# A latent-attention and pooling block: per-token factors as rows, queries and keys of three head pairs kept on chip, first chunk by halves

## The chip, the cores and the metric

The kernel runs on one core of one Trainium2 chip. The metric is the device time of one execution in microseconds (us). The core's engines each run their own stream of instructions in order: TensorE (PE, with weight loads shown as PEld), VectorE (DVE), ScalarE (ACT), GpSimd (POOL) and SyncE (SP, whose queue issues nearly all DMAs). They wait for each other on semaphores.

## What is computed

One encoder layer on 1024 tokens of width 1024, in float32. The parts:

```python
def reference(x, norm_in, w_in, q_norm, w_uq, kv_norm, w_ukv, pool_w, pool_scale,
              w_branch_attn, w_branch_pool, w_out, norm_final):
    h = x
    for _ in range(DEPTH):
        hn = rms_norm(h, norm_in)
        z = jnp.einsum('bsd,de->bse', hn, w_in)
        zq, zkv, zkr, g_attn, u_pool, g_pool, g_merge = jnp.split(z, IN_SPLITS, axis=-1)
        y_attn = mla_attention(zq, zkv, zkr, q_norm, w_uq, kv_norm, w_ukv) * jax.nn.silu(g_attn)
        y_pool = multiscale_pool(u_pool, pool_w, pool_scale) * jax.nn.silu(g_pool)
        a = jnp.einsum('bsc,cd->bsd', y_attn, w_branch_attn)
        p = jnp.einsum('bsc,cd->bsd', y_pool, w_branch_pool)
        gate_a, gate_p = jnp.split(jax.nn.sigmoid(g_merge.astype(jnp.float32)).astype(h.dtype), 2, axis=-1)
        merged = gate_a * a + gate_p * p
        h = h + jnp.einsum('bsd,de->bse', merged, w_out)
    return rms_norm(h, norm_final)
```

`mla_attention` takes the normed latents zq (384 wide) and zkv (256 wide), makes for 8 heads queries and keys of 64 columns each ("nope") and 32 rotary columns, and attends causally by chunks of 64 tokens. `rms_norm` divides each token by its root mean square and multiplies by a gain.

## The kernel before

Every array on chip has features in its 128 partitions and the 1024 tokens in its columns (up to the last stage). A float32 product is made of three products of rounded parts: each operand is split into a high part (a ScalarE cast) and a low part (a VectorE subtraction, helper `split`), and PE adds high times high, high times low and low times high.

**What sets the order.** Nothing is issued where the code stands. The code records operations with the tiles that they read and write in a `Plan` (L85 to 206); `Plan.order` then schedules them by a model of costs, and each engine gets its stream in that order. Of the operations of an engine that could start within 30 ns of the first one, it takes the one recorded earliest. A row of a stream waits only for what it uses, but nothing passes a row that waits. SBUF tiles of 4 KB in each partition come from 45 slots of tag "t" and are handed out in the order of the code; raw weights of the small items have one buffer (tag "wr"), split weights two (tags "wh", "wl"). Each DMA of SP's queue takes one of eight completion semaphores in turn, so at most eight are under way.

**The stages** (times of the profiled execution):

- Up to about 58 us: eight warm-up matmuls, then the latents zq from eight chunks of the features (loop over `ORDER`, L604), each chunk with three products for two halves of the tokens and three column groups. A chunk is `x`; for the first four chunks `xa` holds the gain-scaled high and low part of tokens 0 to 511, `xb` those of the others; the first chunk is loaded and split by halves. Then the rotary key (`run_kr`) and zkv (`run_zkv`).
- `tokens` (L712) turns the sums of squares of the tokens, which lie in a [128 x 8] cell (token 128c + p in row p, column c), into a factor for each token. `spread` (L668) makes of such a cell a [128 x 1024] tile that has each token's factor in every partition: eight PE transposes of one column, broadcast to 128x128, into two PSUM banks. For `rstd`, ScalarE copies the banks to SBUF.
- 71 to 350 us: the rest of the input projection, in `Pair` items (seven products of a Strassen scheme each, 12 matmuls of 512 columns a product). Their weights `w_z` are split beside them. In the last gate pair stand two `Latents` items: they load zq and zkv back, multiply them by their tokens' factors (`spread`, straight from PSUM) and split them.
- 340 to 394 us: `run_up` makes queries and keys of a head pair p = 0 to 3 (64 + 64 partitions), split into `uh` and `ul`. These are stored to DRAM (`qn_d`, `kn_d`), and `load_head` loads the 64 rows of a head from there into the operand tiles `qh`, `ql`, `kh`, `kl` (rows 0 to 63; 64 to 95 rotary from `qr_d` and `kr_d`, 96 to 127 a mask). There are two such sets of tiles, `heads[h % 2]`; head 0's rows come straight from the tiles. `run_rope` and `run_v` follow.
- 394 to about 567 us: attention, head by head: scores `sc`, exponentials `pr` (ScalarE, with the row sums in `small`), transposes `pt`, their split `pT`, products `o` and their copies `oa`. Between them, as filler for PE, stand the products `pf` of the pooling branch (`run_branch_p`): weights `w_bp`, one of eight at a time into `wr`, cast to `wh`, rest to `wl`.
- Then the attention branch, the output projection in pieces, and `Rows.finish` (L1289), which scales the rows by their norm and stores them.

Of the kernel before, what the change touches and what calls it, by code (L numbers as in the profile page):

```python
# [14 lines left out]
P = 128  # L15
# [6 lines left out]
KV_RANK = 256  # L22
N_BG = 4
WARM = 8
# [185 lines left out]
def hybrid_block_kernel(  # L210
# [42 lines left out]
    def dram(rows, name, cols=T):  # L253
        b = Buf(lambda: tc.dram_tile([rows, cols], F32, name=name), None)
        return View(b, 0, rows, 0, cols)
# [219 lines left out]
    qr_d = [[dram(P, f"qr_d{t}{i}") for i in range(2)] for t in range(2)]  # L475
    qn_d = [[dram(P, f"qn_d{p}{i}") for i in range(2)] for p in range(4)]
    kn_d = [[dram(P, f"kn_d{p}{i}") for i in range(2)] for p in range(4)]
    gate_d = [dram(P, f"gate_d{t}") for t in range(16)]
# [125 lines left out]
    for n, k in enumerate(ORDER):  # L604
# [22 lines left out]
        h, l = xs[k]  # L627
        for a, b, f, e in ((wh, h, n == 0, False), (wh, l, False, False), (wl, h, False, n == 7)):
            for hf in range(2):
                mms([(zq_acc[c].halves[hf], a[:, 128 * c : 128 * c + 128], b[hf], f, e) for c in range(3)])  # L630
    for n in range(4):
# [35 lines left out]

    def spread(t, kind=None):  # L668
        acc = Acc(kind) if kind else next_acc()
        transposes(  # L670
            [
                (
                    acc.halves[c // 4][:, 128 * (c % 4) : 128 * (c % 4) + 128],
                    t[:, c : c + 1].via(lambda a: a.to_broadcast([P, P])),
                )
                for c in range(8)
            ]
        )
        return acc

# [31 lines left out]
    def tokens():  # L712
        ts(v_tok, v_tok, 1.0 / D, EPS, ALU.mult, ALU.add)
        inv_sqrt(r_tok, v_tok)
        a = spread(r_tok, "of")
        r = t32("rstd")
        for ps, c, d in a.spans:
            acopy(r[:, c:d], ps)
        state["r"] = r
        norm_tok("q", QK_DIM / Q_RANK, QK_DIM * EPS)  # L720
# [16 lines left out]
    class Latents:  # L737
# [4 lines left out]

        def load(self):
            self.z = [t32("z" + self.key) for _ in z_d[self.key]]
            for z, d in zip(self.z, z_d[self.key]):
                dma(z, d)

        def split(self):
            f = spread(f_tok[self.key], "of")
            for z in self.z:  # L750
                for ps, a, b in f.spans:
                    tt(z[:, a:b], z[:, a:b], ps, ALU.mult)
            state["c" + self.key] = [split_tile(z) for z in self.z]
# [57 lines left out]
    def load_head(h):  # L811
        d = heads[h % 2]
        p, r = h // 2, 64 * (h % 2)
        load_rope(h)
        for x, n in enumerate("hl"):
            dma(d["q" + n][0:64, :].f32(), qn_d[p][x][r : r + 64, :])
            dma(d["k" + n][0:64, :].f32(), kn_d[p][x][r : r + 64, :])

    def run_up(p, which, first):
        def run(it):  # L820
# [18 lines left out]
            for ps, a, b in acc.spans:  # L839
                split(h[:, a:b], l[:, a:b], ps)  # L840
            dst = qn_d if which == "q" else kn_d
            if p == 0:
# [3 lines left out]
                dma(heads[0][which + "l"][0:64, :].f32(), l[0:64, :].f32())  # L846
            r = 64 if p == 0 else 0
            dma(dst[p][0][r:P, :], h[r:P, :].f32())
            dma(dst[p][1][r:P, :], l[r:P, :].f32())
        return run  # L850
# [299 lines left out]
    gate_pair(12, [(3, Rotary())])  # L1150
    gate_pair(14, [(3, q), (5, kv)])
    for n, it in enumerate(i for i in items if isinstance(i, Pair)):
# [104 lines left out]
    class Rows:  # L1257
# [31 lines left out]
        def finish(self, e, last=False):  # L1289
# [12 lines left out]
            elif last:  # L1302
                act(r, r, AF.Copy, scale=st)
            else:
                stt(r, r, st, nf, ALU.mult, ALU.mult)
# [295 lines left out]
```

## Time and profile before

| | |
|---|---|
| three runs | 701.85, 703.6, 706.39 us; median 703.6 |
| profiled execution | 702.37 us |
| its span, first to last instruction | 700.2 us |
| mean granted clock of TensorE | 0.991 of full speed |
| busy: PE, DVE, ACT, POOL | 682.6, 539.6, 355.9, 116.8 us |
| moved by DMA | 136.42 MB |

The span is what the rows below lie in, with times from its start; 2.2 us of the profiled execution lie outside. An engine that is busy for nearly all of the span sets its length, up to the holes in its stream; where an engine waits, the row gives the idle time and what ended it. The clock is the share of full speed that PE was granted.

### The profile page before, as it was taken

How to read it: one execution, taken by the hardware profiler on the slowest of the kernel's cores; microseconds unless marked ns; L12 is line 12 of the kernel's file. 1: busy time of each engine (PE TensorE's matmuls, PEld its weight loads, DVE VectorE, ACT ScalarE, POOL GpSimd, SP SyncE). 2: the span in 40 equal slices, each digit the busy share in tenths (PEclk: the TensorE clock that was granted, in tenths of full speed). 3: DMA queues.
4: the chain of work that ended last, by engine and by line, in shares of the span. 5: the costliest groups of instructions: out<-in, count | busy, mean ns of one | idle time of the engine just before them, and what ended most of it. 6: DMA issues, size and time to landing. Idle time of an engine off the chain costs nothing.

```text
span 700.2 us, 9698 instructions
## 1 busy us (share of the span) xinstructions
PE 682.6 (97%) x3368; PEld 574.3 (82%) x3368; DVE 539.6 (77%) x868; ACT 355.9 (51%) x660; POOL 116.8 (17%) x153
## 2 busy tenths in 40 slices
PE   8999999999999999999999979999999999999995
PEld 6878888888888888888888769999899888878784
DVE  5687997668878578669958757877887889967883
ACT  5864524442444354443545546677676673334433
POOL 0020100300003030300001034444444300000000
PEclk9999999999999999999999989999999999999998
DMA  8947656361977539364778982554540389984612
GB/s 314 383 163 278 208 208 189 82 189 59 316 238 191 176 126 321 85 191 149 293 240 301 331 190 62 147 145 112 122 121 31 106 288 372 303 270 134 203 68 90
DMA packets 55871, 136.42 MB, mean 195 GB/s; under 512 B 5904, under 2 KB 17296, under 8 KB 55696
## 3 DMA queue, kind: packets, MB, share of 16 engines
q1 hardware_dynamic: 53568, 131.63, 56.0%
q0 software_dynamic: 2256, 4.20, 4.2%
q8 instruction: 26, 0.43, 0.3%
q14 instruction: 21, 0.17, 0.1%
HBM read 93.73 MB, written 46.27 MB: 200 GB/s over the span
## 4 chain that ended last, share of the span: by engine, by line
PE 88%; DMA 4%; DVE 3%; issue 2%; ACT 1%; SPq 1%; DVEq 0%; ACTq 0%
PE pb L275 36%; PE ps L275 31%; PE sc L275 6%; PE pf L275 5%; PE o L275 5%; PE pt L282 4%; PE pv L275 2%; DMA kh<-kr_d 1%; DMA wr<-w_bp 1%; SPq L378 1%; DMA x<-xT 1%; DVE mr L308 1%; DMA mr<-m_d 1%; DVE small L357 0%; DVE res L308 0%
## 5 line engine op out<-in xcount | busy, mean ns | idle before, releaser
L275 PE MATMUL pb<-t,wp 128*128 128x512 f32 x504 | 121.3, 389 | 0.0
L275 PEld LDWEIGHTS pb<-t,wp 128*128 128x128 f32 x504 | 94.4, 188 | 19.5
L298 ACT CAST wp<-wr 128x512 fp32r<-128x512 f32 x98 | 59.4, 620 | 94.6 <-PE ps L275 53.3
L308 DVE TENSOR_TENSOR wp<-wr,wp 128x512 fp32r<-128x512 f32 x98 | 71.9, 747 | 36.8 <-ACT wp L298 35.5
L275 PE MATMUL ps<-xa,wp 128*128 128x512 f32 x224 | 73.8, 389 | 0.0
L322 POOL TENSOR_SCALAR pr<-pr,small 128x128 f32<-128x128 f32 (+3 forms) x64 | 48.7, 765 | 77.3 <-DVE small L348 68.9
L290 ACT ACTIVATE pr<-sc,small 128x128 f32<-128x128 f32 (+3 forms) x64 | 47.6, 745 | 19.3 <-DVE small L357 16.4
L308 DVE TENSOR_TENSOR pT<-pt,pT 128x512 fp32r<-128x512 f32 (+1 forms) x80 | 48.8, 633 | 8.9 <-ACT pT L298 8.3
L357 DVE TENSOR_REDUCE small<-sc 128x1 f32<-128x128 f32 (+3 forms) x64 | 47.3, 750 | 9.8 <-PE sc L275 9.2
L298 ACT CAST pT<-pt 128x512 fp32r<-128x512 f32 (+1 forms) x80 | 41.5, 544 | 25.5 <-PE pt L282 24.5
L275 PE MATMUL o<-pT,v 128*128 128x256 f32 (+1 forms) x320 | 48.4, 286 | 2.0 <-ACT pT L298 1.5
L275 PEld LDWEIGHTS ps<-xa,wp 128*128 128x128 f32 x224 | 42.0, 188 | 8.7
L275 PEld LDWEIGHTS o<-pT,v 128*128 128x128 f32 x320 | 44.8, 193 | 4.8 <-ACT pT L298 1.9
L275 PE MATMUL ps<-xb,wp 128*128 128x512 f32 x112 | 43.6, 389 | 0.0
L282 PE MATMUL pt<-ident,pr 128*128 128x128 f32 x288 | 42.6, 276 | 0.3 <-DVE pT L308 0.3
L275 PE MATMUL pb<-wo,wp 128*128 128x512 f32 (+1 forms) x180 | 40.5, 376 | 0.2 <-DVE res L308 0.2
L275 PE MATMUL pb<-xa,wp 128*128 128x512 f32 x168 | 40.7, 389 | 0.0
L275 PE MATMUL ps<-t,wp 128*128 128x512 f32 x168 | 40.7, 390 | 0.0
L275 PE MATMUL sc<-kh,qh 128*128 128x384 f32 (+4 forms) x96 | 36.2, 377 | 2.9 <-ACT pr L290 2.8
L275 PEld LDWEIGHTS pb<-wo,wp 128*128 128x128 f32 x180 | 32.4, 188 | 7.0 <-issue 0.5
L275 PEld LDWEIGHTS pb<-xa,wp 128*128 128x128 f32 x168 | 31.5, 188 | 6.5
L275 PEld LDWEIGHTS ps<-t,wp 128*128 128x128 f32 x168 | 31.5, 188 | 6.5
(207 smaller groups left out, 1446.5 us busy)
## 6 DMA issues: line engine op xcount, KB each, us to landing
wr<-w_z SPq DMA_DIRECT2D x30, 512.0 KB, 5.3
gate_d<-z SPq DMA_DIRECT2D x16, 512.0 KB, 3.5
xt<-xr SPq DMA_DIRECT2D x8, 512.0 KB, 9.8
mp<-gate_d SPq DMA_DIRECT2D x8, 512.0 KB, 6.5
gate<-gate_d SPq DMA_DIRECT2D x8, 512.0 KB, 7.4
wo<-wt_d SPq DMA_DIRECT2D x8, 512.0 KB, 9.2
m_d<-gate SPq DMA_DIRECT2D x16, 256.0 KB, 5.7
mr<-m_d SPq DMA_DIRECT2D x16, 256.0 KB, 4.5
```

The source lines that it names most:

```text
L275: nc.tensor.matmul(real(o), real(a), real(b), start=s, stop=e, **kw)
L282: nc.tensor.transpose(real(o), real(a), real(ident))
L290: nc.scalar.activation(real(o), real(x), func, scale=real(scale), **kw)
L298: lambda: nc.scalar.copy(real(o), real(x)),
L308: plan.add(eng, lambda: e.tensor_tensor(real(o), real(a), real(b), op), c, [a, b], [o], port=port)
L322: e.tensor_scalar(real(o), real(a), real(s1), real(s2), op0, op1)
L357: lambda: nc.vector.tensor_reduce(real(o), real(a), axis=AX.X, op=ALU.max, negate=True),
L378: lambda: nc.sync.dma_start(real(o), real(x)),
```

## The change

Four things change.

1. `spread` makes one transpose of the [128 x 8] cell to [8 x 128], a ScalarE copy to a small tile `eight`, a store of its 4 KB to a new row in DRAM, and a load that repeats that row to all 128 partitions of a "t" tile. `rstd`, `fq` and `fkv` are made so, and multiplied with from SBUF, 1024 columns at a time. For a latent this now happens when it is loaded, not when it is split, and q stands one product earlier in the last gate pair.
2. For head pairs 0 to 2 (`KEPT`) `uh` and `ul` stay in their "t" tiles, and `load_head` copies from there; pair 3 goes through DRAM as before.
3. In the first chunk the loop over halves is outermost.
4. One of the last two row scalings moves from ScalarE to VectorE.

```diff
--- before.py
+++ after.py
@@ -20,7 +20,7 @@
 QK_DIM = 96
 Q_RANK = 384
 KV_RANK = 256
-N_BG = 4
+KEPT = 3
 WARM = 8
 SLOTS = {"t": 45, "wr": 1, "wh": 2, "wl": 2, "go": 2, "oa": 2, "s": 2, "p": 2, "o": 1, "f": 1}
 PSUM = "spof"
@@ -473,8 +473,8 @@
     mask_d = dram(64, "mask_d")
     kr_d = [dram(32, f"kr_d{i}") for i in range(2)]
     qr_d = [[dram(P, f"qr_d{t}{i}") for i in range(2)] for t in range(2)]
-    qn_d = [[dram(P, f"qn_d{p}{i}") for i in range(2)] for p in range(4)]
-    kn_d = [[dram(P, f"kn_d{p}{i}") for i in range(2)] for p in range(4)]
+    n_d = {w: [dram(P, f"{w}n_d{i}") for i in range(2)] for w in "qk"}
+    nope = {}
     gate_d = [dram(P, f"gate_d{t}") for t in range(16)]
     y_d = [dram(P, f"y_d{t}") for t in range(4)]
     gp_d = [dram(P, f"gp_d{t}") for t in range(4)]
@@ -625,9 +625,11 @@
         if n + 3 < 8:
             raws[ORDER[n + 3]] = start_loads(ORDER[n + 3])
         h, l = xs[k]
-        for a, b, f, e in ((wh, h, n == 0, False), (wh, l, False, False), (wl, h, False, n == 7)):
-            for hf in range(2):
-                mms([(zq_acc[c].halves[hf], a[:, 128 * c : 128 * c + 128], b[hf], f, e) for c in range(3)])
+        parts = ((wh, h, n == 0, False), (wh, l, False, False), (wl, h, False, n == 7))
+        for (a, b, f, e), hf in (
+            [(p, hf) for hf in range(2) for p in parts] if n == 0 else [(p, hf) for p in parts for hf in range(2)]
+        ):
+            mms([(zq_acc[c].halves[hf], a[:, 128 * c : 128 * c + 128], b[hf], f, e) for c in range(3)])
     for n in range(4):
         B.setdefault("b11", []).append((xs[n][0][0], xs[n][1][0]))
         B.setdefault("b21", []).append((xs[4 + n][0][0], xs[4 + n][1][0]))
@@ -665,18 +667,17 @@
         act(o, x, AF.Sqrt)
         recip(o, o)
 
-    def spread(t, kind=None):
-        acc = Acc(kind) if kind else next_acc()
-        transposes(
-            [
-                (
-                    acc.halves[c // 4][:, 128 * (c % 4) : 128 * (c % 4) + 128],
-                    t[:, c : c + 1].via(lambda a: a.to_broadcast([P, P])),
-                )
-                for c in range(8)
-            ]
-        )
-        return acc
+    def spread(t, name):
+
+        ps = Acc("of").halves[0]
+        transposes([(ps[:8, :P], t)])
+        eight = buf("oa", 256, F32, "eight")[:8, :P]
+        acopy(eight, ps[:8, :P])
+        d = dram(1, name)
+        dma(d.via(lambda a: a.rearrange("a (c p) -> (a c) p", c=8)), eight)
+        o = t32(name)
+        dma(o, d.via(lambda a: a.rearrange("a c -> (a c)").partition_broadcast(P)))
+        return o
 
     f_tok = {"q": cell(8), "kv": cell(8)}
     zq, zkv = [], []
@@ -712,11 +713,7 @@
     def tokens():
         ts(v_tok, v_tok, 1.0 / D, EPS, ALU.mult, ALU.add)
         inv_sqrt(r_tok, v_tok)
-        a = spread(r_tok, "of")
-        r = t32("rstd")
-        for ps, c, d in a.spans:
-            acopy(r[:, c:d], ps)
-        state["r"] = r
+        state["r"] = spread(r_tok, "rstd")
         norm_tok("q", QK_DIM / Q_RANK, QK_DIM * EPS)
 
     def run_zkv(j):
@@ -741,15 +738,14 @@
             self.key = key
 
         def load(self):
+            self.f = spread(f_tok[self.key], "f" + self.key)
             self.z = [t32("z" + self.key) for _ in z_d[self.key]]
             for z, d in zip(self.z, z_d[self.key]):
                 dma(z, d)
 
         def split(self):
-            f = spread(f_tok[self.key], "of")
             for z in self.z:
-                for ps, a, b in f.spans:
-                    tt(z[:, a:b], z[:, a:b], ps, ALU.mult)
+                tt(z, z, self.f, ALU.mult)
             state["c" + self.key] = [split_tile(z) for z in self.z]
 
         def go(self, it):
@@ -813,8 +809,8 @@
         p, r = h // 2, 64 * (h % 2)
         load_rope(h)
         for x, n in enumerate("hl"):
-            dma(d["q" + n][0:64, :].f32(), qn_d[p][x][r : r + 64, :])
-            dma(d["k" + n][0:64, :].f32(), kn_d[p][x][r : r + 64, :])
+            for w in "qk":
+                dma(d[w + n][0:64, :].f32(), nope[w, p][x][r : r + 64, :])
 
     def run_up(p, which, first):
         def run(it):
@@ -838,15 +834,17 @@
             h, l = tr("uh"), tr("ul")
             for ps, a, b in acc.spans:
                 split(h[:, a:b], l[:, a:b], ps)
-            dst = qn_d if which == "q" else kn_d
             if p == 0:
                 if which == "q":
                     make_slots()
                 dma(heads[0][which + "h"][0:64, :].f32(), h[0:64, :].f32())
                 dma(heads[0][which + "l"][0:64, :].f32(), l[0:64, :].f32())
-            r = 64 if p == 0 else 0
-            dma(dst[p][0][r:P, :], h[r:P, :].f32())
-            dma(dst[p][1][r:P, :], l[r:P, :].f32())
+            if p < KEPT:
+                nope[which, p] = h.f32(), l.f32()
+            else:
+                nope[which, p] = n_d[which]
+                for v, o in zip((h, l), n_d[which]):
+                    dma(o, v.f32())
         return run
 
     def run_rope(t):
@@ -1148,7 +1146,7 @@
     silu_pair(4, ga_d[2:4])
     gate_pair(10)
     gate_pair(12, [(3, Rotary())])
-    gate_pair(14, [(3, q), (5, kv)])
+    gate_pair(14, [(2, q), (5, kv)])
     for n, it in enumerate(i for i in items if isinstance(i, Pair)):
         for j, f in enumerate(hooks.get(n, [])):
             it.after[1 + 3 * j] = f
@@ -1300,7 +1298,7 @@
                 stt(r[:, 256:512], r[:, 256:512], st, nf[:, 256:512], ALU.mult, ALU.mult)
                 ts(r[:, :256], r[:, :256], st, None, ALU.mult)
             elif last:
-                act(r, r, AF.Copy, scale=st)
+                ts(r, r, st, None, ALU.mult)
             else:
                 stt(r, r, st, nf, ALU.mult, ALU.mult)
             for c in (lft, rgt):
```

**Where the instructions come to stand.** First PE's stream at its beginning: the 18 matmuls of the first chunk (`xa` holds the high and the low part of half 0, `xb` those of half 1, `wqh` and `wql` are the weights' parts; of the three accumulators `ps_130` and `ps_132` hold both halves, `pb_134` and `pb_146` one each). The piece of difference:

```order
 L275 MATMUL ps_132<-xa_121,wqh_126 128x512
 L275 MATMUL pb_134<-xa_121,wqh_126 128x512
+L275 MATMUL ps_130<-xa_121,wql_128 128x512
+L275 MATMUL ps_132<-xa_121,wql_128 128x512
+L275 MATMUL pb_134<-xa_121,wql_128 128x512
 L275 MATMUL ps_130<-xb_136,wqh_126 128x512
 L275 MATMUL ps_132<-xb_136,wqh_126 128x512
 L275 MATMUL pb_146<-xb_136,wqh_126 128x512
-L275 MATMUL ps_130<-xa_121,wql_128 128x512
-L275 MATMUL ps_132<-xa_121,wql_128 128x512
-L275 MATMUL pb_134<-xa_121,wql_128 128x512
 L275 MATMUL ps_130<-xb_136,wql_128 128x512
 L275 MATMUL ps_132<-xb_136,wql_128 128x512
```

The first nine matmuls, three with `xa`, three with `xb` and three with `xa` again (its low part), keep their order; behind them the three with `wql` for half 0 go ahead of the three for the low part of half 1.

Next SP's stream where attention begins, at the second load of `w_bp` into `wr` (the keys of the last pair are `uh_3179` and `ul_3191` before, `uh_3141` and `ul_3153` after), before:

```order
L378 DMA kn_d_3161<-uh_3146 128x1024
L378 DMA kn_d_3164<-ul_3148 128x1024
L378 DMA kn_d_3166<-uh_3150 128x1024
L378 DMA kn_d_3177<-ul_3153 128x1024
L378 DMA wr_3193<-w_bp 128x512
L378 DMA kn_d_3197<-uh_3179 128x1024
L378 DMA kn_d_3210<-ul_3191 128x1024
L378 DMA qh_3289<-mask_d 32x1024
```

and after:

```order
L378 DMA kl_3092<-kr_d_2663 32x1024
L378 DMA qn_d_3103<-ul_3075 128x1024
L378 DMA mp_3105<-gate_d_2265 128x1024
L378 DMA kl_3092<-ul_3088 64x1024
L378 DMA wr_3155<-w_bp 128x512
L378 DMA kn_d_3159<-uh_3141 128x1024
L378 DMA kn_d_3172<-ul_3153 128x1024
L378 DMA qh_3253<-mask_d 32x1024
```

Between the first load of `w_bp` and this second one stand nine issues now, seventeen before; what is gone are stores of `uh` and `ul`. The last pair's two key stores follow it in both. Then come head 1's ten loads, and behind them the third load of `w_bp`, before:

```order
L378 DMA ga_3299<-ga_d_2092 128x1024
L378 DMA qh_3289<-qr_d_3013 32x1024
L378 DMA ql_3293<-qr_d_3027 32x1024
L378 DMA qh_3289<-qn_d_2945 64x1024
L378 DMA kh_3291<-kn_d_3113 64x1024
L378 DMA ql_3293<-qn_d_2962 64x1024
L378 DMA kl_3295<-kn_d_3141 64x1024
L378 DMA wr_3359<-w_bp 128x512
L378 DMA qh_2928<-qr_d_3013 32x1024
```

and after:

```order
L378 DMA kh_3257<-uh_3077 64x1024
L378 DMA ql_3261<-qr_d_3005 32x1024
L378 DMA ql_3261<-ul_2912 64x1024
L378 DMA kl_3265<-kr_d_2663 32x1024
L378 DMA kl_3265<-ul_3088 64x1024
L378 DMA ga_3269<-ga_d_2087 128x1024
L378 DMA wr_3299<-w_bp 128x512
L378 DMA wr_3367<-w_bp 128x512
L378 DMA qh_2914<-qr_d_2991 32x1024
```

Head 1's rows 0 to 63 come from `uh` and `ul` and no longer stand at the end; the gate's load comes behind them, and the fourth load of `w_bp` follows the third at once.

Last ACT's stream at the same place: `wh<-wr` is the cast of a `w_bp` weight, `pr<-sc` an exponential, `pT<-pt` the cast of transposed probabilities, before:

```order
L298 CAST v_3287<-pv_3260 128x8x64
L290 ACT_TABLE_LOAD
L290 ACTIVATE pr_3323,small<-sc_3275,small 128x128
L290 ACTIVATE pr_3325,small<-sc_3279,small 128x256
L298 CAST wh_3334<-wr_3193 128x512
L298 CAST pT_3357<-pt_3348 128x384
L290 ACTIVATE pr_3364,small<-sc_3327,small 128x384
L290 ACTIVATE pr_3370,small<-sc_3336,small 128x512
L298 COPY oa_3386<-o_3374 64x256
```

and after:

```order
L298 CAST hi_3235<-y_2857 128x1024
L298 CAST wh_3246<-wr_3155 128x512
L298 CAST v_3251<-pv_3222 128x8x64
L290 ACT_TABLE_LOAD
L290 ACTIVATE pr_3287,small<-sc_3237,small 128x128
L290 ACTIVATE pr_3291,small<-sc_3241,small 128x256
L298 CAST pT_3321<-pt_3314 128x384
L290 ACTIVATE pr_3326,small<-sc_3293,small 128x384
L290 ACTIVATE pr_3332,small<-sc_3302,small 128x512
L298 CAST wh_3341<-wr_3299 128x512
L298 COPY oa_3350<-o_3336 64x256
```

The cast of the second weight now stands ahead of the table load and the exponentials, no longer ahead of `pT`; that of the third stands where attention's fourth exponential has been issued, ahead of `oa`.

## Rows read from the trace of the kernel before

**Rows 1.** The page, busy time of the engines: us, share of the span, instructions.

```profile
PE 682.6 (97%) x3368; PEld 574.3 (82%) x3368; DVE 539.6 (77%) x868; ACT 355.9 (51%) x660; POOL 116.8 (17%) x153
```

**Rows 2.** What PE waited for: total us, times, longest us.

```profile
PE sc L275 <- ACT pr L290: 2.8, 2, 2.0
PE o L275 <- ACT pT L298: 1.5, 1, 1.5
```

**Rows 3.** Timeline of ACT, first head: start, us, instruction, [idle before <-releaser].

```profile
394.94 1.28 ACT L290 ACT_TABLE_LOAD   x1
...
402.99 0.62 ACT L298 CAST wh<-wr 128x512 fp32r<-128x512 f32 x1 [4.93 <-DMA wr<-w_bp]
403.52 0.47 ACT L298 CAST pT<-pt 128x384 fp32r<-128x384 f32 x1
...
415.22 0.62 ACT L298 CAST wh<-wr 128x512 fp32r<-128x512 f32 x1 [3.55 <-DMA wr<-w_bp]
```

**Rows 4.** Timeline of PE, the same stretch, the rows with waits.

```profile
404.04 0.38 PE L275 MATMUL o<-pT,v 128*128 128x256 f32 x1 [1.53 <-ACT pT L298]
404.86 0.90 PE L275 MATMUL o<-pT,v 128*128 128x256 f32 x3 [0.43 <-DVE pT L308]
...
417.40 0.33 PE L275 MATMUL sc<-kh,qh 128*128 128x128 f32 x1 [1.97 <-ACT pr L290]
```

**Rows 5.** Stretches: us, busy of five engines, PEclk, DMA share, GB/s.

```profile
396.00:398.00 2.00, 2.00 (x10) 1.68 (x9) 1.58 (x5) 1.11 (x5) 0.05 (x1) 1.00 1.02 399
...
404.00:406.00 2.00, 1.53 (x6) 1.33 (x7) 1.61 (x5) 1.44 (x5) 1.00 (x2) 0.68 0.87 221
406.00:408.00 2.00, 2.00 (x9) 2.00 (x8) 0.93 (x3) 0.17 (x1) 0.28 (x1) 0.50 0.75 215
...
418.00:420.00 2.00, 2.00 (x7) 1.42 (x7) 2.00 (x4) 0.31 (x1) 0.86 (x1) 0.60 1.05 213
420.00:422.00 2.00, 2.00 (x12) 2.00 (x11) 1.38 (x3) 1.18 (x2) 0.00 (x0) 0.55 1.02 199
...
440.50:443.00 2.50, 2.50 (x17) 2.12 (x16) 1.68 (x6) 2.13 (x6) 1.85 (x2) 1.00 1.07 206
```

**Rows 6.** Timeline of SP's queue, the second and the third load of w_bp.

```profile
392.93 1.07 SPq L378 DMA_DIRECT2D wr<-w_bp  x1
...
407.52 0.53 SPq L378 DMA_DIRECT2D wr<-w_bp  x1
```

**Rows 7.** DMA issues, whole run: KB each, median us from issue to landing.

```profile
wr<-w_bp SPq DMA_DIRECT2D x8, 256.0 KB, 4.4
...
qh<-qn_d SPq DMA_DIRECT2D x7, 256.0 KB, 3.9
...
zq<-zq_d SPq DMA_DIRECT2D x3, 512.0 KB, 5.2
...
qh<-uh SPq DMA_DIRECT2D x1, 256.0 KB, 5.3
...
kr_d<-krh SPq DMA_DIRECT2D x1, 128.0 KB, 1.9
```

**Rows 8.** Timeline of PE, spread of the factors of q.

```profile
332.43 1.04 PE L282 MATMUL pb<-ident,small 128*128 128x128 f32 x8
333.22 2.99 PE L275 MATMUL pb<-t,wp 128*128 128x512 f32 x12
```

**Rows 9.** Timeline of DVE: use of rstd, of q's factors, last split of keys.

```profile
82.46 0.69 DVE L308 TENSOR_TENSOR z<-z,rstd 128x512 f32<-128x512 f32 x1
...
333.83 3.67 DVE L308 TENSOR_TENSOR zq<-zq,pb 128x512 f32<-128x512 f32 x6
...
384.24 1.28 DVE L308 TENSOR_TENSOR ul<-pb,uh 128x512 fp32r<-128x512 f32 x2
```

**Rows 10.** Timeline of PE, first chunk.

```profile
7.85 0.73 PE L275 MATMUL ps<-xb,wqh 128*128 128x512 f32 x2 [1.29 <-ACT xb L290]
```

**Rows 11.** Timeline of ACT, the last rows.

```profile
693.28 1.15 ACT L290 ACTIVATE res<-res,small 128x1024 f32<-128x1024 f32 x1 [0.23 <-DVE small L348]
```

## The prediction

> **What bounds the kernel now.** I read the page first, then the list of what PE waits for, then the timelines around the longest of those waits. TensorE is busy 682.6 of 700.2 us [rows 1], so only two things can shorten the span: fewer or faster PE instructions, or fewer holes in PE's stream. VectorE and ScalarE have slack on average, and a saving there counts only where PE waits for it. The list of PE's waits [rows 2] names ScalarE's `pr` (2.8 us) and `pT` (1.5 us) in attention as the largest two; the rest of the list is single waits of 1.4 us or less, one of them in the first chunk.
>
> The two holes in attention are not ScalarE being busy. Read [rows 3] from the left: at 402.99 ScalarE casts `wh<-wr` after 4.93 us of idleness released by the DMA `wr<-w_bp`; only then comes `pT<-pt` (403.52), which PE's `o` was waiting for. At 415.22 the same cast ends another 3.55 us of idleness, and PE's `sc` waits behind it for the next `pr`. So a weight for the filler product (`pf`) stands in ScalarE's in-order queue ahead of the work that attention needs, and that weight is late because of the DMA. PE pays 1.53 + 0.43 us at the first place and 1.97 us at the second [rows 4]. It pays again afterwards: in the stretches after the holes the granted clock is 0.68 and 0.50, then 0.60 and 0.55, where it was 1.00 before [rows 5]; that is the 1.2 GHz level for part of each stretch, with PE busy all of it in three of the four.
>
> Why the weight is late: its loads are issued at 392.93 and 407.52 [rows 6] and land about 10 us and 7.6 us later, against a median of 4.4 us [rows 7]. Just then the 16 DMA engines are full: 1.02 of their time at 399 GB/s in 396 to 398 [rows 5]. What fills them are the copies of the head-pair queries and keys to DRAM, and SP issues everything in one order, so the loads stand behind them in its queue too.
>
> **The change, part by part.** *Spread.* Eight 128x128 transposes became one, in three places. The eight take 333.22 − 332.43 = 0.79 us of PE from start to next start [rows 8]; one of eight is 0.1 us. Saving 0.69 us, three times: **−2.1 us**, all on PE's path. The first spread no longer needs two ScalarE copies; ten VectorE products from PSUM (the six for q take 3.67 us, 0.61 each, [rows 9]) become five of 1024 columns in SBUF. Both engines wait for others at those places, so I count nothing for them.
> The price is latency: a small store, then a 512 KB load that repeats a row. No repeating load is in the trace; the nearest rows are a small store at 1.9 us and an ordinary 512 KB load at 5.2 us [rows 7], so 7.1 us from the copy to the rows, with no reason to be below the store alone (1.9 us) and, with the load twice as slow, 12.3 us. I take 7.1, as the load has an ordinary load's bytes to write. What hides it: for q the load now stands one product earlier (2 in place of 3) and the planner sends the transpose ahead of the rotary key's stores. The list of issues puts the rows' load in front of the `zq` loads that VectorE needs as well, so it lands about when `zq` does, at 331 to 332, against a first use at 333.83 before [rows 9]. For kv the use comes with the key products, long after. For the first spread the rows are first used by VectorE at 82.46 [rows 9]; stored at about 62 they are there by 70. The waiting instruction is SP's second one, which holds some 2 us of later issues (chunk reloads, first `w_z`) whose users have a few us left. I book 0 here, and take −0.2 to +2 us as bounds.
>
> *First chunk.* The code now runs half 0 through all its parts before half 1. That could hide the wait of 1.29 us for `xb` ahead of 7.85 [rows 10] behind six more matmuls, about 6 × 0.23 = 1.4 us. But the order shows that the planner still sets the first product of half 1 second: the first nine matmuls stand as before, and only two groups of three swap behind them. The wait stays: **0**.
>
> *Queries and keys kept.* For pairs 0 to 2 the stores to DRAM go (twelve issues, 4 × 256 KB + 8 × 512 KB, 5.2 MB); heads 0 to 5 read the tiles from SBUF. Only pair 3 is still stored. At the 399 GB/s of [rows 5], 5.2 MB is 13 us of all 16 engines, between 358 and 396. Between the first `w_bp` load and the second stand nine issues in place of seventeen, and the second's cast on ScalarE stands before the table load, ahead of the first exponentials, not ahead of `pT`. The buffer is free once VectorE has split the first one, just before the last `ul`, which ended at 384.24 + 1.28 = 385.5 [rows 9]. Issued then and landing in 4.4 to 6 us, it is there by 390 to 392, and the cast must be through before the table load, which started at 394.94 [rows 3]. **First hole: gone**, with 2 to 4 us to spare.
> The third load is the closer call. Ahead of it in SP's queue now stand the ten loads of head 1 (4 × 256 KB and 6 × 128 KB, 1.8 MB) and a 512 KB gate. Loads of 64 or 32 partitions run at 206 GB/s with the engines at 1.07 [rows 5], so 1.8 MB takes 8.7 us; begun at about 388, they are through by 397, the gate by 398.5, and `w_bp` lands at 399 to 401.5. ScalarE needs it after the exponentials of 384 and 512 columns, at about 402 in a stream without the first hole. The fourth load follows directly, so the second hole's cause (a load issued behind head 1's copies at 407.52) goes also. **Second hole: gone**, but with 0.5 to 3 us to spare.
> Worth of the holes: waits 1.53 + 0.43 + 1.97 = 3.93 us. Clock: PE at a granted share g for a stretch of 2 us does 2g us of work; lost are 0.5 (404 to 406, where PE was busy 1.53 at 0.68), 1.0 (406 to 408), 0.8 and 0.9 (418 to 422) [rows 5], 3.2 us. Together **−7.1 us**. The lost clock is a consequence of the holes in both places, so I let it go with them.
> The head loads themselves gain nothing: `qh<-uh` from SBUF takes 5.3 us, `qh<-qn_d` from DRAM 3.9 [rows 7].
> The tiles now live longer in the 45 slots of tag "t". By the order of emission 43 of them are held at most where attention begins (39 before), so nothing waits for a slot there.
>
> *Tail.* The last rows' scaling, 1.15 us on ScalarE [rows 11], moves to VectorE, about 0.7 us there, before the last product's sum. Two short engines trade: −0.1 us.
>
> Sum: −2.1 − 7.1 − 0.1 = −9.3 us. The profiled execution took 702.37 us, so 693.1; the median of the three is 703.6, 1.2 above it, so **694.3**.
>
> **The rivals.** *(A) The third load stays late.* Head 1's copies now take the place of the stores in front of it. For it: at 206 GB/s they are slow, and I have 0.5 to 3 us to spare. Against it: 5 MB fewer are under way. The ScalarE cast would again stand ahead of an `oa` copy and an exponential, and the second hole with its clock remains: 1.97 + 1.7 = 3.7 us come back, 698. The stretch at 206 GB/s [rows 5] is one of loads into partitions 0 to 63. The Trainium skill, SBUF — State Buffer, section "Door 1: The DMA port swizzle", states that such a transfer reaches half of the ports (about 218 GB/s) and one into 64 to 127 the other half. [...]
> *(B) The holes stay.* Something else than the stores makes `w_bp` late (a slot, SP's limit of eight loads under way), and just the transposes count: −2.2, about 701.4. For it: the buffer `wr` is single, and its release by VectorE was not far ahead of the issue. Against it: the 4.93 us of idleness end with the DMA's landing, and the queue was full.
> *(C) Slower: the repeating load for q is late.* The first query products need all of `fq` before any latent can be split, and nothing else is ready for PE at 340, when the last pair is done. A load that reads one 4 KB row 128 times might be served one read after the other: 4 KB at a sixteenth of 206 GB/s take 0.32 us, 128 of them 41 us. It decides from about 3 us of lateness on; each us beyond counts one for one, and the clock falls after the hole. To end above 703.6 it must eat the 9.3 us: it would have to land 12 us after its due time; say 20 us late, 703.6 − 9.3 + 17 = 711. Against it: the ordinary 512 KB load, also 128 rows of 4 KB, takes 5.2 us in all [rows 7], so rows are not moved one by one there. The Trainium skill, DMA: Bandwidth & Descriptors, section "Why a DMA increments its semaphore by 16 and not by 1", states that the number of engines follows from the outermost sizes of the two sides, here 128 copies and 128 partitions: all 16 engines. No row here shows a repeating load.
> *(D) The first chunk does what it says* would give 1.3 more, 693.0; the order excludes it.
>
> **How the numbers follow.** Within 1% means 696.6 to 710.6, about what a measurement of this kernel can tell from no change. Forecast, both holes gone: 0.64, 691 to 697. A: 0.18, 696 to 699. B: 0.13, 700 to 702.5. C: 0.05, 704 to 720, most of it above 710.6. Low end of the range: the forecast less the spread of the runs, which lie up to 1.8 below the median, and less another 2 for small waits that go unseen: 690.0. High end: what lies above may hold most of B and C, some 0.15 together: 700.5. Faster by over 1%: nearly all of the forecast and a little of A, 0.66. Within 1%: A, B and a bit of the rest, 0.30. Slower by over 1%: the far part of C, 0.04.
>
> **What would show it.** In the profile after: at the three spreads one transpose, and the products before and behind 0.1 us apart; PE's wait for `xb` at 7.9 us still 1.3; no `wh<-wr` cast with a DMA as releaser between 395 and 420, the waits of `o` for `pT` and of `sc` for `pr` gone, and granted clock 1.00 through 400 to 425; the DMA share between 375 and 400 clearly under 1. It is wrong if a new wait stands in place of these: `pr` or `oa` behind a cast that waits for the third `w_bp` (A), PE before the query products waiting for a `hi` or `lo` of `zq` (C), or VectorE waiting for `rstd` near 80 us.

## The result and the profile after

The changed kernel took 695.08 us (median of four runs, 694.62 to 698.27) against 703.55 before, ratio 0.9886, interval 0.9849 to 0.9923. Measured twice more beside the kernel before, on other occasions, it stood at 0.9937 (0.9911 to 0.9963; 698.41 against 703.27) and at 0.9925 (0.990 to 0.9949; 697.17 against 702.32). So the kernel is faster, by 4.9 to 8.5 us. The forecast was −9.3 us (694.3): the first measurement lies 0.8 us above it, and by the other two it was 4 us too good. The profiled execution of the changed kernel took 698.27 us, the longest of the four; its span is 696.5 us.

The page, its first line and the busy line: 21 PE matmuls fewer (three times seven transposes), and PE still has no slack.

```profile
span 696.5 us, 9669 instructions
...
PE 678.7 (97%) x3347; PEld 569.2 (82%) x3347; DVE 540.2 (78%) x864; ACT 354.8 (51%) x660; POOL 116.0 (17%) x153
```

What PE waited for after the change (total, times, longest), to be read against [rows 2]: the 2.0 us for `pr` and the 1.5 us for `pT` are gone, but three waits are new, for `z`, for `ul` and for `wp`. The first two are in all three profiles of the changed kernel, the third in this one alone.

```profile
PE pb L275 <- DVE z L308: 1.6, 1, 1.6
PE pre L275 <- DVE zero L457: 1.4, 1, 1.4
PE ps L275 <- ACT xb L290: 1.2, 1, 1.2
PE pb L275 <- DVE ul L308: 1.2, 1, 1.2
PE pb L275 <- ACT wp L298: 1.1, 1, 1.1
PE sc L275 <- ACT pr L290: 0.8, 1, 0.8
```

ScalarE where attention begins, answering to [rows 3]: the cast of the second `w_bp` weight (395.86) stands ahead of the table load and waits for no DMA; that of the third (403.88) doesn't either.

```profile
395.86 0.62 ACT L298 CAST wh<-wr 128x512 fp32r<-128x512 f32 x1
...
396.98 1.28 ACT L290 ACT_TABLE_LOAD   x1
...
402.03 0.48 ACT L298 CAST pT<-pt 128x384 fp32r<-128x384 f32 x1 [2.48 <-PE pt L282]
...
403.88 0.62 ACT L298 CAST wh<-wr 128x512 fp32r<-128x512 f32 x1
```

The stretches that answer to [rows 5]: PE busy throughout at a granted clock of 1.00, and DMA engines with time to spare from 404 to 408 (shares of 0.00 and 0.39).

```profile
404.00:406.00 2.00, 2.00 (x16) 1.97 (x15) 1.88 (x4) 0.87 (x2) 0.88 (x2) 1.00 0.00 0
406.00:408.00 2.00, 2.00 (x14) 1.83 (x13) 1.37 (x3) 1.53 (x3) 0.54 (x1) 1.00 0.39 131
...
418.00:420.00 2.00, 2.00 (x15) 1.78 (x15) 1.20 (x5) 1.42 (x5) 1.85 (x4) 1.00 1.02 199
420.00:422.00 2.00, 2.00 (x13) 1.79 (x11) 1.75 (x4) 0.78 (x2) 0.59 (x1) 1.00 0.51 199
```

To see where the time came from, I divide PE's timeline at three instructions that each trace has: the first matmul of the second chunk, the first `pf` of attention (with its wait for `v`), and a late `pt` of attention. Of the kernel before:

```profile
11.38 0.62 PE L275 MATMUL ps<-xa,wqh 128*128 128x512 f32 x2
...
395.20 0.50 PE L275 MATMUL pf<-hi,wh 128*128 128x512 f32 x1 [0.28 <-DVE v L308]
...
556.53 0.52 PE L282 MATMUL pt<-ident,pr 128*128 128x128 f32 x3 [0.28 <-DVE pT L308]
```

and of the kernel after:

```profile
11.49 0.62 PE L275 MATMUL ps<-xa,wqh 128*128 128x512 f32 x2
...
396.72 0.50 PE L275 MATMUL pf<-hi,wh 128*128 128x512 f32 x1 [0.29 <-DVE v L308]
...
550.92 0.52 PE L282 MATMUL pt<-ident,pr 128*128 128x128 f32 x3 [0.28 <-DVE pT L308]
```

The stages are the differences of these starts; the last is the rest of the span. Every kernel of the study is in the table, each by its one profile.

| kernel | to chunk 2 | projections | attention | rest | span |
|---|---|---|---|---|---|
| before | 11.4 | 383.8 | 161.3 | 143.7 | 700.2 |
| after | 11.5 | 385.2 | 154.2 | 145.6 | 696.5 |
| after, second profile | 13.1 | 385.1 | 153.8 | 144.6 | 696.6 |
| after, third profile | 10.6 | 385.0 | 153.8 | 144.7 | 694.2 |
| kept_only | 13.5 | 384.0 | 153.7 | 143.5 | 694.7 |
| spread_only | 13.3 | 385.3 | 161.3 | 145.1 | 705.0 |
| dead_unseen | 10.4 | 385.0 | 162.0 | 145.4 | 702.7 |
| kv_early | 10.6 | 392.8 | 153.8 | 145.7 | 703.0 |
| kv_z_first | 10.5 | 388.0 | 153.5 | 144.1 | 696.2 |
| warm29 | 13.5 | 382.5 | 153.8 | 144.2 | 694.0 |
| nine | 10.8 | 385.3 | 153.6 | 144.6 | 694.3 |
| early_rows | 13.2 | 383.9 | 153.6 | 144.1 | 694.8 |
| kept_nine | 10.7 | 383.9 | 153.8 | 144.5 | 692.8 |
| best2 | 12.8 | 381.5 | 153.7 | 143.7 | 691.7 |

Attention gave 7.1 to 7.5 us. The projections, where PE has three times seven transposes less, became 1.2 to 1.4 us longer, not 2.1 shorter: 3.3 to 3.5 us came back there. The rest became 0.9 to 1.9 us longer. The first column differs by up to 2.5 us between profiles of one kernel, and that is no part of the change.

### The profile page after: what moved, and what is told of

Read it like the earlier page. It is cut to its first block, busy times and chain, and to the rows that moved or that the text cites. A ratio compares the mean times of both kernels' runs of the same rounds, so it can differ in the third digit from the quotient of the medians.

```text
span 696.5 us, 9669 instructions
## 1 busy us (share of the span) xinstructions
PE 678.7 (97%) x3347; PEld 569.2 (82%) x3347; DVE 540.2 (78%) x864; ACT 354.8 (51%) x660; POOL 116.0 (17%) x153
## 4 chain that ended last, share of the span: by engine, by line
PE 77%; DMA 9%; DVE 8%; issue 2%; ACT 2%; SPq 0%; DVEq 0%; ACTq 0%
PE pb L275 30%; PE ps L275 25%; PE sc L275 7%; PE pf L275 6%; PE o L275 5%; PE pt L282 4%; DMA wr<-w_ba 3%; DMA m_d<-gate 1%; DVE gate L308 1%; DMA wr<-w_uv 1%; PE pv L275 1%; DMA zkv<-zkv_d 1%; DVE wo L308 1%; DMA x<-xT 1%; DVE lo L308 1%
## 5 line engine op out<-in xcount | busy, mean ns | idle before, releaser
L308 DVE TENSOR_TENSOR pT<-pt,pT 128x512 fp32r<-128x512 f32 (+1 forms) x80 | 48.8, 633 | 10.4 <-ACT pT L298 9.4
L275 PE MATMUL o<-pT,v 128*128 128x256 f32 (+1 forms) x320 | 47.0, 281 | 0.0
L282 PEld LDWEIGHTS pt<-ident,pr 128*128 128x128 f32 x288 | 32.8, 141 | 4.4 <-issue 0.9
```

Source lines behind the costliest of these rows:

```text
L275: nc.tensor.matmul(real(o), real(a), real(b), start=s, stop=e, **kw)
L282: nc.tensor.transpose(real(o), real(a), real(ident))
L308: plan.add(eng, lambda: e.tensor_tensor(real(o), real(a), real(b), op), c, [a, b], [o], port=port)
```

## The two new waits

The wait for `z` starts at the row of kv's factors. SP's timeline:

```profile
335.59 0.28 SPq L378 DMA_DIRECT2D fkv<-eight  x1
338.35 0.32 SPq L378 DMA_DIRECT2D fkv<-fkv  x1
338.76 1.07 SPq L378 DMA_DIRECT2D zkv<-zkv_d  x2
```

SP issues the 4 KB store at 335.59 and stands until it has landed; the repeating load goes at 338.35 and the loads of `zkv` at 338.76, where the kernel before issued them at 334.81. VectorE then waits for them:

```profile
345.20 1.23 DVE L308 TENSOR_TENSOR zkv<-zkv,fkv 128x1024 f32<-128x1024 f32 x1 [2.96 <-DMA zkv<-zkv_d]
```

Behind this product in VectorE's queue stand the last evacuations of the last pair's banks (`z`), and PE wants such a bank for the third query product:

```profile
351.69 0.50 PE L275 MATMUL pb<-hi,wh 128*128 128x512 f32 x1 [1.56 <-DVE z L308]
```

The wait for `ul` near 377 goes back to the weight `w_uv`. ScalarE after the change, where the kernel before had it at 372.81 after 4.48 us idle:

```profile
374.66 1.05 ACT L298 CAST wh<-wr 128x1024 fp32r<-128x1024 f32 x1 [6.54 <-DMA wr<-w_uv]
```

The load was issued at 367.66, at the same point of the work as before, but its cast began 7.0 us later in place of 4.9 (372.81 after an issue at 367.87). The DMA view of 366 to 375 has one row that the same stretch of the kernel before lacks, a 16 KB packet of queue 8, instructions:

```profile
q1 hardware_dynamic: 475, 1.69, 56.2%
q8 instruction: 1, 0.02, 1.0%
```

1.0% of 16 engines' 9 us is about 1.4 us on one engine. Queue 8 has 26 such packets in a run. My reading was that they are PE's instructions: with 21 matmuls fewer, the same instruction number comes 21 matmuls later, and a load that used to be over before `w_uv` was issued now falls into it. That is tested below.

Each of these waits costs PE more than its own length, as the matmuls behind it start slower. From 349.75 to 352.03 PE gets through two matmuls that take 0.45 us elsewhere, and from 376.99 to 380.16 through six that took 1.35 us in the kernel before (377.30 to 378.65): 1.8 us each, 3.6 together. The three transposes save 3 × 0.76 = 2.3 us. That leaves +1.3 us, which is what the projections show.

The wait for `wp` (620.59, in the output projection) has a load behind it that reads back a store, too: SP stood 3.1 us for a store of `m_d` before it issued the loads `mr` at 616.89; in the second profile it stood 2.0 us, and PE didn't wait. As kept_nine below, which has no rows, has 0.6 us of this wait, it does not belong to the rows.

## The experiments

**kept_only.** The kernel before with the second part of the change alone (`n_d`, `nope`, `KEPT`; no rows, no halves, the scaling on ScalarE).

> The kernel before with only the queries and keys of three pairs kept on chip. Theory H (the stores made the second and third w_bp load late): both holes of attention go, -6 to -7 us against the kernel before, ratio 0.990 to 0.992, clock 1.00 through 400 to 425, and no wait of VectorE for zkv near 345. Rival O (the planner's new places for the casts do it together with the spread's new order): less than 4 us of it, ratio above 0.994, and one of the holes stays.

Measured: 696.36 us against 703.27, ratio 0.9904 (0.9871 to 0.9936). Attention 153.7 us, projections 384.0, no wait for `z` or `ul`. Theory H holds, and this part alone gives what the whole change gives, as far as the intervals tell.

**spread_only.** The kernel before with the first part alone:

```diff
+        transposes([(ps[:8, :P], t)])
+        acopy(eight, ps[:8, :P])
+        dma(d.via(lambda a: a.rearrange("a (c p) -> (a c) p", c=8)), eight)
+        dma(o, d.via(lambda a: a.rearrange("a c -> (a c)").partition_broadcast(P)))
```

> The kernel before with only the factors as rows (and q one product earlier). Theory H: -2.1 us of transposes, of which +1.6 come back as VectorE waits for zkv behind the row's store in SP's queue; both holes of attention stay as they were: -0.5 us, ratio 0.998 to 1.001. Rival S (the rows cost nothing, the wait in the profile after belongs to the stores that are gone): -2.1 us, ratio 0.997 or below, no wait of PE for z near 350.

Measured: 708.78 us against 703.27, ratio 1.0096 (1.0059 to 1.0133): slower, by more than I had expected. Its profile has both waits, 1.7 us for `z` and 1.0 for `ul`, and attention at 161.3 as before (its holes lie in other places; one of 5.33 us). The projections are 1.5 us longer than before; the other 3.3 us of its span are 1.9 in the first chunk and 1.4 in the rest (0.9 of it the wait for `wp`), which vary in other kernels too. Rival S falls. That the rows cost more than they save is shown; that they cost all of 5.5 us is not.

**dead_unseen.** The changed kernel with the twelve stores back in SP's queue, read by nobody and without cost in the planner's model:

```diff
+                r = 64 if p == 0 else 0
+                for x, v in zip("hl", (h, l)):
+                    dma(dram(P, f"dead_{which}{p}{x}")[r:P, :], v[r:P, :].f32())
+                    plan.ops[-1].bytes = 1
```

> The changed kernel, with the twelve stores of pairs 0 to 2 put back into SP's queue as stores that nobody reads, at a cost of nothing in the planner's model, so that ScalarE's casts keep the places that they have after the change. Theory H: the traffic is the cause, so the second w_bp load lands near 400 again and its cast, now ahead of the first exponentials, stops PE for at least as long as before: +5 to +10 us on the changed kernel, ratio to the kernel before 0.995 to 1.005. Rival O (the cast's place is what counts): no more than +2 us, ratio below 0.992.

Measured: 705.36 us against 703.27, ratio 1.0054 (1.0025 to 1.0083), 7 us above the changed kernel beside it (698.41), attention 162.0. The second `w_bp` load is issued at 392.91 again, and the cast that stands ahead of the table load waits for it:

```profile
399.93 0.62 ACT L298 CAST wh<-wr 128x512 fp32r<-128x512 f32 x1 [5.35 <-DMA wr<-w_bp]
```

PE's stop there is longer than either of the two before:

```profile
402.86 0.69 PE L275 MATMUL sc<-kh,qh 128*128 128x384 f32 x1 [4.50 <-ACT pr L290]
```

So the stores made the holes; the cast's new place with the stores still there is a loss. Rival O falls. Whether the stores do it by their bytes or by their places in SP's queue this run doesn't separate. The place counts for much: the second load goes at 385.87 in the changed kernel and at 392.93 before, and it comes in time although the DMA engines are still busy for 0.95 of 375 to 400 (0.98 before).

**after_again** and **after_third.** The changed kernel, for a second and third profile.

> The changed kernel once more, for a second profile and more times. If the wait of 1.6 us for z at 350 comes from SP's queue, it is there again, within 0.5 us; if the wait of 1.2 us for ul at 377 comes from a straggling packet of the w_uv load, it is gone, and the time is 694.5 to 696. A rival (both are in every execution) gives both waits and 697 to 699.

> The changed kernel once more beside these, for a comparison on one chip: ratio 0.989 to 0.993 to the kernel before, with the waits for z near 350 (1.4 to 1.6) and for ul near 377 (1.2) in its profile.

Both waits were there both times, 1.4 for `z` and 1.1 to 1.2 for `ul`, at 698.41 and 697.17 us: the straggling packet is in all three profiles, so my first guess, that it was chance, fell. The wait for `xb` in the first chunk was 1.0 in one and absent in the other.

**kv_early** (`(4, kv)` in place of `(5, kv)`) and **kv_z_first** (the loads of `zkv` recorded ahead of the row's).

> The changed kernel with the kv latents one product earlier (4 in place of 5). If the wait of 1.4 to 1.6 us for z near 350 comes from the kv rows landing late (store, then SP held until it has landed, then loads), 2.7 us more lead remove it: no wait of PE for z, VectorE's wait for zkv under 0.5 us. A rival (VectorE has too much to do there, whatever lands when) leaves at least 1 us. The wait near 377 stays in either.

> The changed kernel with the loads of zkv ahead of the load of its factor rows in SP's queue. If SP standing behind the row's store is what makes zkv late (2.7 us), zkv lands as early as in the kernel before, the rows land last, and VectorE's wait of 3.0 us shrinks by 1 to 2.5 us, PE's from 1.4 to 1.6 us to under 0.8. A rival (the repeating load itself is slow) leaves both waits within 0.4 us, now with fkv as the releaser.

Both missed, in one run each (704.8 and 697.97 us, beside one of the kernel before at 707.18). In kv_early SP issued the `zkv` loads only 1.0 us earlier (337.72), and the planner moved VectorE's products forward with them, so VectorE waited as long (3.2 us), and PE waited 4.2 us for `z` in the middle of the last pair. In kv_z_first `zkv` was issued at 334.99, early as before, but the row's load only at 338.72, as the store took 4.1 us to release SP; it landed last, 6.4 us later, VectorE waited 3.5 us for `fkv` and PE 2.5 for `z`. My reading was that the store must come earlier, and that who stands behind whom in the 3 us after it only changes the name of the wait. early_rows tests that.

**early_rows.** The transposes and stores of q's and kv's rows made where their factors are ready (stores issued at 68.69 and 84.36); only the repeating loads stay:

```diff
-            self.f = spread(f_tok[self.key], "f" + self.key)
+            self.f = spread(f_row[self.key], "f" + self.key)
+                f_row["kv"] = store_row(f_tok["kv"], "fkv")
```

> The changed kernel with the rows of q and kv transposed and stored near 65 to 80 us, when their factors are ready, so that at 320 to 340 only the repeating load is left. If the hold of SP behind the store (2.7 to 3.7 us) makes zkv late, VectorE's wait for zkv falls from 2.5 to 3.0 us to under 0.8, PE's wait of 1.4 to 1.6 for z near 350 to under 0.5; the wait near 377 for w_uv stays: -1 to -1.6 us on the changed kernel. A rival (the extra 512 KB load alone makes it late) leaves 1 us or more of PE's wait.

Measured: PE's wait for `z` is gone; VectorE's for `zkv` is 1.6 us (more than the 0.8 expected) and costs PE nothing; `ul` stays with 1.3. The projections are 383.9, 1.2 us less than in the changed kernel. The time, 695.4 us (0.9904, 0.9869 to 0.9939), can't be told from the changed kernel's by its interval.

**warm29.** 29 warm-up matmuls of 128 columns for 8 of 512, so that PE has as many instructions as before:

```diff
-    for _ in range(WARM):
-        mms([(pre, zero[:, :P], zero, True, True)])
-        plan.ops[-1].cost = 427
+    for _ in range(WARM + 21):
+        mms([(pre[:, :P], zero[:, :P], zero[:, :P], True, True)])
+        plan.ops[-1].cost = 118
```

> The changed kernel with 29 warm-up matmuls of 128 columns in place of 8 of 512: 21 more PE instructions at the start, as many as the transposes that are gone, in about the same time. If the wait of 1.2 us for ul near 377 is PE's 16 KB code load sharing a DMA engine with the w_uv load (it starts at 371 to 374 in the kernels with one transpose, at 365.5 to 366 in those with eight), the code load moves back ahead of the w_uv load, w_uv lands in under 5.2 us and PE's wait there is gone. A rival (the w_uv load is slow because of what else the change put into the queues) leaves w_uv at 6.5 to 7 us and the wait at 1.0 us or more.

Measured: no wait for `ul` at all, and ScalarE gets `w_uv` as early as in the kernel before:

```profile
373.61 1.05 ACT L298 CAST wh<-wr 128x1024 fp32r<-128x1024 f32 x1 [4.45 <-DMA wr<-w_uv]
```

Nothing near `w_uv` was edited, only the count of PE's instructions. All nine profiles with 3347 PE matmuls have the wait (1.0 to 1.3 us), all five with 3368 lack it. The projections fall to 382.5; the small warm-up matmuls take 2.1 us longer than the eight, though (PE's first product at 7.70 in place of 5.6). One run: 695.81 us. The wait for `z` fell too, to 0.7 us, with SP held 2.8 us behind the store as in the changed kernel (337.56 to 340.40). So the store is not all of that wait. A 16 KB packet lies between 336 and 340 in the changed kernel's three profiles, beside the store and the loads, and between 334 and 336 here, ahead of them; that it is the other part is not shown.

**nine.** The nine matmuls of half 0 of the first chunk as one operation:

```diff
-            mms([(zq_acc[c].halves[hf], a[:, 128 * c : 128 * c + 128], b[hf], f, e) for c in range(3)])
+            mms([(zq_acc[c].halves[hf], a[:, 128 * c : 128 * c + 128], b[hf], f, e)
+                 for (a, b, f, e), hf in group for c in range(3)])
```

> The changed kernel with the nine matmuls of half 0 of the first chunk bound into one operation, so that the planner can't put half 1 between. If the wait of 1.0 to 1.3 us (1.7 at most) for xb is only a question of what stands ahead of it, it falls to under 0.4 us and the first chunk ends 0.8 to 1.3 us earlier. A rival (the low part of half 0, or the weights' low part, is as late as xb) gives the same wait under another name, gain under 0.3 us.

Measured: half 1 starts nine matmuls later and hardly waits:

```profile
8.09 0.40 PE L275 MATMUL pb<-xa,wql 128*128 128x512 f32 x1
8.50 0.73 PE L275 MATMUL ps<-xb,wqh 128*128 128x512 f32 x2
```

The second chunk begins at 10.8 here (696.06 us in one run) and at 10.7 in kept_nine; in the kernels without it (and without the longer warm-up) between 10.4 and 13.5, since the wait for `xb` is 0 to 1.7 us from one profile to the next. After the three longest (1.6 to 1.7 us) matmuls take 0.63 us in place of 0.40; in kept_only the granted clock from 10 to 12 is 0.50, the 1.2 GHz level. So the edit would do what its words say, if the planner let it. In the three profiles that have it the bad case doesn't occur; its worth in time is not shown.

**kept_nine** (kept_only and nine) and **best2** (the changed kernel with early_rows, warm29 and nine, the last scaling back on ScalarE).

> The kernel before with only the kept queries and keys and the nine matmuls as one, none of the rows. Against the kept part alone (694.0 to 697.1) -1 us: 694 to 695.5, ratio 0.987 to 0.990. If the rows are worth anything once their waits are gone, it stays 1.5 to 2.5 us behind the kernel with all that the runs pointed to; a rival (the rows are worth nothing) puts it within 0.5 us of that or ahead.

> All that the runs pointed to: the changed kernel with early rows, the code load moved ahead by 29 small warm-up matmuls, the first chunk's nine matmuls as one, and the last scaling back on ScalarE. If the three waits add up, -1.5 (z) -1.6 (ul) -1.0 (xb) = about -4 us on the changed kernel: 691 to 693, ratio to the kernel before 0.982 to 0.987. A rival (the waits are given back at the next late load) ends within 1.5 us of the changed kernel.

kept_nine took 693.27 us, ratio 0.9867 (0.9845 to 0.9889); best2 694.97 us, 0.9886 (0.9865 to 0.9906); the changed kernel beside them 697.17. So both beat the changed kernel, by 3.9 and 2.2 us; best2's interval just touches the changed kernel's, but its slowest run (695.19) is below the other's fastest (695.38). best2 missed its 691 to 693. The kernel without any rows is 1.7 us ahead of it, which the intervals don't separate; the rows are at any rate not worth the 1.5 to 2.5 us that they should bring once their waits are gone. best2's profile has neither `z` nor `ul` nor `xb` among PE's waits, its projections are the shortest of all (381.5) and 2.4 us shorter than kept_nine's, of which the warm-up takes 2.1 back. Its profiled execution was the fastest of its six (693.47); the five others, of which only the span is known, are 2.0 us behind kept_nine's in the median (694.99 against 693.0). Where those lose it stays open.

## Why the prediction came out as it did

*Kept tiles, −7.1.* Right in what it gave: attention is 7.1 us shorter in the first profile, 7.5 in the other two, 7.6 with this part alone; the clock came back with the holes. Two of its steps did not go as worked out. The sign "the DMA share between 375 and 400 clearly under 1" did not come (0.95, before 0.98): the second load is in time because it is issued 7 us earlier, not because the engines are free. And the third load, which I had landed by 399 to 401.5 behind head 1's loads, was issued only at 399.59, when VectorE had done with the one `wr` buffer:

```profile
398.84 0.68 DVE L308 TENSOR_TENSOR wl<-wr,wh 128x512 fp32r<-128x512 f32 x1
399.59 6.18 SPq L378 DMA_DIRECT2D wr<-w_bp  x2
```

SP waited 2.4 us for that. The cast at 403.88 still found its weight, as ScalarE came to it 2 us later than I had it; in warm29 and best2 the same cast waits 1.0 us for the load, at no cost to PE. That the second hole closed was thus in part luck: a term was missing in its sum, the hold by the buffer.

*Spread, −2.1.* The transposes went as worked out: one takes 0.27 us, and the next product starts 0.03 us after it. The step that failed is "For kv the use comes with the key products, long after", with the 0 booked for latency. The first use is VectorE's product, and what stands behind it in VectorE's queue is the release of PE's bank, not the key products. It was 1.4 to 1.6 us of waiting and 1.8 us of PE's time, inside my bound of 2. Rival C is a near relation: a late load holds PE, but at kv and not at q, and by the store ahead of it, not by the repeating. Also too small: 1.9 us for the store, taken from a 128 KB one; SP stood 2.5 to 4.1 us behind 4 KB. The repeating load itself is no dearer than an ordinary one: `rstd<-rstd` took 4.1 us, against 5.2 for `zq<-zq_d` [rows 7]. By the Trainium skill, DMA: Bandwidth & Descriptors, section "Why a DMA increments its semaphore by 16 and not by 1", a load whose two sides both begin with 128 runs on all 16 engines; this time agrees with that.

*What no step had.* 1.2 us for `ul`, 1.8 us of PE's time with the slower start: 21 PE instructions fewer moved a 16 KB code load into the load of `w_uv`, which had no room for it.

*First chunk, 0.* Right, the wait stayed where the order had it (1.17 us); that it varies by itself between 0 and 1.7 us I did not know, and it blurs every single profile.

*Tail, −0.1.* Wrong in sign, small: from the last but one reciprocal to the last sum of squares it is 690.24 − 688.87 = 1.37 us now, 694.34 − 693.08 = 1.26 before, as VectorE's scaling stands ahead of the last sum.

So −7.3 in attention, +1.3 in place of −2.1 in the projections, and +0.9 to +1.9 in the rest. Of the 1.9 in the first profile 1.1 is the wait for `wp`; but for that and the tail, the rest's cause stays open (it varies by 1 us between kept_only and kept_nine too). Together some −4 to −5 us, which the second and third measurement show. That the first one gave −8.5 and so came within 0.8 us of the forecast is luck: nothing in its own profile, 3.7 us shorter in span, bears it out. Its interval overlaps with the others', so it may be no more than the scatter of the runs.

*The range.* The forecast less 1.8 and less 2 is 690.5, not 690.0.

## What to carry to other kernels

A gain off one engine is judged at the queue it hands its latency to: find the first instruction that uses the new value, and then who waits for what stands behind it. Where a value goes through DRAM, make the store as soon as the value exists; here SP stood behind a store that a load reads back even when it was 4 KB. When a change alters an engine's instruction count, its code loads move; look whether one now falls into a weight load without slack.

## What the runs showed of the hardware

A 4 KB store to DRAM held the load that reads it back for 2.5 us (61.73 to 64.19, DMA share 0.42) to 4.1 us (334.61 to 338.72 in kv_z_first, DMA share 0.99). A 16 KB instruction packet occupied one DMA engine for about 1.4 us, and a 512 KB load that shared the engines with it was there 2 us later; with 3347 PE matmuls PE's wait behind it came in all nine profiles, with 3368 in none of five. While head 1's last loads, into partitions 0 to 63 or 64 to 127, and the gate's were under way, the DMA engines were full (share 1.04 in 396 to 400) at 238 to 242 GB/s, where the kernel before moved 399 in 396 to 398.
